# First waits tile by tile, attention's scores two tiles ahead, and the next head's q and k split early

## The chip, the core and the metric

The kernel runs on one core of one Trainium2 chip. The metric is the device time of one execution in microseconds (us). TensorE (PE in the profile) multiplies, VectorE (DVE), ScalarE (ACT) and GpSimd (POOL) work element by element, and SyncE (SP) issues nearly all DMAs. Each engine takes its instructions in the order in which they stand in its queue, and waits at an instruction until the semaphores that it names have been raised.

## What is computed

One inference step of a two-layer decoder: a gated linear attention (GLA) layer and a differential attention layer, each with a squared-ReLU MLP, for a prompt of 1024 tokens behind 16 meta tokens, and for eight running sequences with a paged cache of 4096 tokens each. The change is about the prompt's differential attention: eight heads, each with two score maps of depth 64 over the same values. Cut to that:

```python
def diff_core(q, k, v, q_pos, k_pos, lam):
    s = jnp.einsum('bqhmd,bkhmd->bhmqk', q, k).astype(F32) * (DIFF_DH ** -0.5)
    mask = k_pos[None, :] <= q_pos[:, None]
    s = jnp.where(mask, s, -jnp.inf)
    p = jax.nn.softmax(s, axis=-1)
    a = p[:, :, 0] - lam * p[:, :, 1]
    return jnp.einsum('bhqk,bkhe->bqhe', a, v.astype(F32))

def diff_prompt(x, w_in, lam, lam_init, g_sub, w_out):
    q, k, v = diff_project(x, w_in, pos)          # projections and partial rope
    ...                                           # diff_core, 128 queries at a time
    out = diff_output(o, g_sub, lam_init, w_out, x.dtype)   # rms_norm per head, then @ w_out
    return out, k.reshape(B, T, DIFF_HEADS, 2 * DIFF_DH), v
```

## The kernel before

**Stages.** In order of time: the GLA layer with the sample tokens' own path; the GLA output projection and the first MLP, beside which the running sequences' paged attention (`decode`, L861) goes on in the background; the projections of q, k and v (L1094 to L1136), still with `decode` beside them; the prompt's differential attention (L1142 to L1273); its output projection and the second MLP. Products keep fp32 accuracy by splitting each operand into a high and a low part (`split`, L194: a copy on ACT writes the high part, a subtraction on DVE or POOL the low one) and running three matmuls (`mm3`, L198). A weight tile comes by DMA into `raw` (L184), ACT casts it into `whi` (L186), and POOL subtracts into `wlo` (L187).

**Pools.** On-chip memory is handed out in pools that are opened and closed stage by stage on the same addresses. A tile's first user must wait for whoever used its memory before. With the default setting, that is everything that used the memory under the whole pool. `open_banks` (L125) does the same for the eight PSUM banks: three `mm`, three `ax` and two `sm` banks elsewhere, in attention two pairs `pr`, two `ax`, two `sm`. Attention opens `a1`, `a2`, `a3` and `scp` (L1144 to L1147) where `decode`'s page buffers (`pg`) and the projections' output buffers (`qo`) lay. Among their tiles are the mask `cmask`, two value tiles for the meta tokens `vm` that POOL clears (L1158), and five score tiles `as` of `scp`.

**One tile of attention** (`tile_`, L169) is 128 queries t = 0 to 7 of one head h against W = 16 + 128(t + 1) keys, in one to three chunks of at most 512 keys. Per chunk PE makes both score maps, three matmuls each (L1187), into a pair of PSUM banks; DVE adds the mask, scales, keeps the running minimum and writes to `as` (L1189), once per map. Over the whole width ACT takes the exponential with its sum (L1191, twice), DVE works out a reciprocal (L1193) and a factor (L1194) and combines the two maps (L1195). Then PE transposes 128 x 128 blocks (L1204, t + 2 of them), ACT copies them out (L1206), and PE multiplies with the values (L1209). A head is eight such tiles and 14 chunks; its next head's q and k are prepared by `prep` (L1075): 17 transposes of the reloaded rows (L1082, L1088), casts on ACT (L195), subtractions on DVE (L196). In a head the tiles come in the order 7, 1, 5, 3, 6, 0, 4, 2, and `prep` is advanced one step at tiles n = 1 to 4 of that order. `load_v` (L1160) loads the next head's values at n = 3, `load_qk` (L1065) the rows of the head after the next at n = 5. Every second head `o_norm` (L1213) scales finished outputs, in the last head `o_fm` (L1225) turns them for the output projection.

**What sets the order.** The program is written tile after tile; a scheduler puts each engine's instructions into a fixed order beforehand, so that some of tile n + 1's scores stand before tile n's transposes. On the chip each queue then runs in that order.

Of the kernel before, what the change touches and what calls it, by code (L numbers as in the profile page):

```python
# [25 lines left out]
NM = 16  # L26
# [9 lines left out]
PGB = 10  # L36
RUN = 4
HOLD = range(212, 228)
HTB = 1
# [72 lines left out]
def hybrid_step(ctx, tc, A, dbg=None, upto=9):  # L112
# [81 lines left out]
    def split(hi, lo, src, eng=V):  # L194
        S.copy(hi, src)  # L195
        return eng.tensor_tensor(lo, src, hi.bitcast(F32), op=ALU.subtract)  # L196
# [538 lines left out]
    kp = ctx.enter_context(tc.tile_pool(name="kp", bufs=1))  # L735
    de = ExitStack()
    dp = de.enter_context(tc.tile_pool(name="dp", bufs=1))
    dp2 = de.enter_context(tc.tile_pool(name="dp2", bufs=2))
    pgp = de.enter_context(tc.tile_pool(name="pgp", bufs=PGB))
# [297 lines left out]
    hp = e.enter_context(tc.tile_pool(name="hp", bufs=1))  # L1037
    ht = e.enter_context(tc.tile_pool(name="ht", bufs=HTB))
# [14 lines left out]
    rp = e.enter_context(tc.tile_pool(name="rp", bufs=1))  # L1053
    qt = e.enter_context(tc.tile_pool(name="qt", bufs=3))
    ht = e.enter_context(tc.tile_pool(name="qht", bufs=2))
# [7 lines left out]
    rqp = er.enter_context(tc.tile_pool(name="rqp", bufs=2, side="right"))  # L1063
# [80 lines left out]
    a1 = e.enter_context(tc.tile_pool(name="a1", bufs=1))  # L1144
    a2 = e.enter_context(tc.tile_pool(name="a2", bufs=4))
    a3 = e.enter_context(tc.tile_pool(name="a3", bufs=6))
    scp = e.enter_context(tc.tile_pool(name="scp", bufs=5))  # L1147
# [21 lines left out]
    def tile_(h, t, out, vm, vx, ks, qs):  # L1169
# [25 lines left out]
        V.scalar_tensor_tensor(sc_[:, 0, :W], sc_[:, 1, :W], neg[:, 0:1], sc_[:, 0, :W], ALU.mult, ALU.add)  # L1195

# [38 lines left out]
    vnxt = load_v(0)  # L1235
    for h in range(8):
        if h:
            head = hnxt
        vh = vnxt
        for n, t in enumerate((3, 2, 1, 0, 7, 6, 5, 4) if h == 7 else (7, 1, 5, 3, 6, 0, 4, 2)):  # L1240
            if h < 7:
                if n == 0:
                    nxt = prep(h + 1, *raws[h + 1])
                elif n < 5:
                    hnxt = next(nxt)
                if n == 3:
                    vnxt = load_v(h + 1)
# [6 lines left out]
            if n % 4 == 3:  # L1254
                ts = (slice(0, 4), slice(4, 8))[n // 4] if h == 7 else slice(t % 2, 8, 2)
                S.copy(Yd[:, ts, h], po.rearrange("p (t e) -> p t e", e=P))
                for i in range(4):
                    x = po[:, i * P : (i + 1) * P]
                    j = ts.start + i * (ts.step or 1)
                    S.activation(x, x, AF.Square, accum_out=oss[:, j, h : h + 1])  # L1260
            if n == 3 and h == 7:
                o_norm(slice(0, 4), slice(7, 8))
                for j in range(8):
                    o_fm(j, 0)
        if h < 6 and h % 2:
            o_norm(slice(0, 8), slice(h - 1, h + 1))
        elif h == 6:
            o_norm(slice(0, 8), slice(6, 7))
# [10 lines left out]
    hp = e.enter_context(tc.tile_pool(name="hp", bufs=1))  # L1279
    ht = e.enter_context(tc.tile_pool(name="ht", bufs=HTB))  # L1280
    rwp = e.enter_context(tc.tile_pool(name="rwp", bufs=5))
# [308 lines left out]
```

## Time and profile before

| | |
|---|---|
| median of 3 runs | 2869.12 us (2863.24, 2869.12, 2870.97) |
| the profiled execution | 2864.1 us, of which the span of its instructions is 2862.3 us |
| PE busy over the span | 2742.9 us, 96% |
| granted TensorE clock, mean | 0.987 |
| attention, first to last score reduction on DVE | 1785.02 to 2031.67 us |

Times in the trace count from the span's start. In rows of the timeline the columns are start, duration, engine (a q behind it is its queue of DMA issues), line, operation, tiles written and read, shape and count; the bracket holds the idle time of that engine before the row and what ended it. Rows of waits give the total, the number of times and the longest. Rows of windows give a stretch from start to end and its length, then the busy time of PE, PEld (loads of stationary operands), DVE, ACT and POOL with their instructions in brackets, the granted TensorE clock as a share of full speed, the DMA engines' busy share and GB/s. Ends of matmuls are modelled, so that a busy PE need not be a PE at its limit.

### The profile page before, as it was taken

How to read it: one execution, taken by the hardware profiler on the slowest of the kernel's cores; microseconds unless marked ns; L12 is line 12 of the kernel's file. 1: busy time of each engine (PE TensorE's matmuls, PEld its weight loads, DVE VectorE, ACT ScalarE, POOL GpSimd, SP SyncE). 2: the span in 40 equal slices, each digit the busy share in tenths (PEclk: the TensorE clock that was granted, in tenths of full speed). 3: DMA queues.
4: the chain of work that ended last, by engine and by line, in shares of the span. 5: the costliest groups of instructions: out<-in, count | busy, mean ns of one | idle time of the engine just before them, and what ended most of it. 6: DMA issues, size and time to landing. Idle time of an engine off the chain costs nothing.

```text
span 2862.3 us, 52240 instructions
## 1 busy us (share of the span) xinstructions
PE 2742.9 (96%) x19849; PEld 2244.1 (78%) x19849; DVE 1947.2 (68%) x3046; ACT 1095.1 (38%) x2229; POOL 1105.9 (39%) x744
## 2 busy tenths in 40 slices
PE   8889999999999999999999999888999999999997
PEld 5666667997777777777799978777889889797985
DVE  2565544568878787777668720788538887878788
ACT  3233344242221221221341112777615546355553
POOL 1221212233344343434233311000226767777774
PEclk9899999999999999999999999999999999999999
DMA  7557741634898898988669993111434555564584
GB/s 250 179 175 267 256 169 44 242 96 156 284 338 296 313 358 295 340 313 316 229 202 321 364 353 100 45 46 31 129 107 85 108 132 115 130 130 111 129 191 89
DMA packets 271833, 560.71 MB, mean 196 GB/s; under 512 B 23559, under 2 KB 138829, under 8 KB 267485
## 3 DMA queue, kind: packets, MB, share of 16 engines
q1 hardware_dynamic: 252284, 520.66, 53.2%
q0 software_dynamic: 19296, 36.71, 8.0%
q8 instruction: 156, 2.56, 0.4%
q14 instruction: 97, 0.79, 0.1%
HBM read 531.16 MB, written 29.26 MB: 196 GB/s over the span
## 4 chain that ended last, share of the span: by engine, by line
PE 74%; DVE 10%; DMA 6%; issue 4%; ACT 4%; POOL 1%; SPq 0%; DVEq 0%; POOLq 0%; ACTq 0%
PE mmt L199 18%; PE mmt L200 17%; PE mmt L201 17%; PE smt L843 4%; PE axt L199 3%; PE axt L200 3%; PE axt L201 3%; ACT as L1191 2%; DMA pg<-in_cache_k 1%; DMA swt<-in_mlp_w 1%; PE smt L519 1%; PE smt L1209 1%; DVE as L1189 1%; DVE Y L1506 1%; PE smt L1453 1%
## 5 line engine op out<-in xcount | busy, mean ns | idle before, releaser
L187 POOL TENSOR_TENSOR wlo<-raw,whi 128x512 fp32r<-128x512 f32 x256 | 365.4, 1440 | 769.9 <-ACT whi L186 688.6
L200 PE MATMUL mmt<-wlo,XH 128*128 128x256 f32 (+1 forms) x1760 | 526.3, 300 | 4.6 <-POOL wlo L187 4.6
L199 PE MATMUL mmt<-whi,XH 128*128 128x256 f32 (+1 forms) x1760 | 525.0, 301 | 4.6 <-ACT Y L323 3.6
L199 PE MATMUL mmt<-XH,whi 128*128 128x512 f32 (+1 forms) x1216 | 435.9, 359 | 5.1 <-DVE Y L913 3.0
L201 PE MATMUL mmt<-whi,XL 128*128 128x256 f32 x1536 | 436.7, 286 | 0.0
L201 PE MATMUL mmt<-XH,wlo 128*128 128x512 f32 (+1 forms) x1216 | 432.1, 356 | 0.0
L186 ACT CAST whi<-raw 128x512 fp32r<-128x512 f32 x256 | 153.0, 620 | 603.2 <-PE mmt L201 196.7
L200 PEld LDWEIGHTS mmt<-wlo,XH 128*128 128x128 f32 x1760 | 333.8, 190 | 32.3 <-issue 16.4
L803 DVE TENSOR_REDUCE sc<-pg 128x16 f32<-128x1024 f32 x256 | 308.3, 1212 | 72.4 <-POOL pg L802 69.8
L199 PEld LDWEIGHTS mmt<-whi,XH 128*128 128x128 f32 x1760 | 332.2, 190 | 30.8 <-issue 13.5
L802 DVE TENSOR_TENSOR pg<-pg,qb 128x1024 f32<-128x1024 f32 x192 | 267.3, 1399 | 62.1 <-DMA pg<-in_cache_k 52.1
L200 PE MATMUL mmt<-XL,whi 128*128 128x512 f32 x768 | 306.4, 399 | 0.0
L201 PEld LDWEIGHTS mmt<-whi,XL 128*128 128x128 f32 x1536 | 290.7, 190 | 8.7 <-issue 8.0
L199 PEld LDWEIGHTS mmt<-XH,whi 128*128 128x128 f32 x1216 | 229.7, 189 | 52.0 <-issue 12.9
L802 POOL TENSOR_TENSOR pg<-pg,qb 128x1024 f32<-128x1024 f32 x64 | 161.8, 2529 | 266.1 <-DMA pg<-in_cache_k 202.8
L201 PEld LDWEIGHTS mmt<-XH,wlo 128*128 128x128 f32 x1216 | 229.8, 189 | 34.4 <-issue 2.1
L199 PE MATMUL mmt<-whi,HH 128*128 128x512 f32 x512 | 205.1, 402 | 5.6 <-DVE Y L1027 5.2
L201 PE MATMUL mmt<-whi,HL 128*128 128x512 f32 x512 | 204.1, 399 | 0.0
L200 PE MATMUL mmt<-wlo,HH 128*128 128x512 f32 x512 | 203.6, 398 | 0.0
L1435 POOL TENSOR_TENSOR wlo<-RW,whi 128x512 fp32r<-128x512 f32 x96 | 173.6, 1843 | 49.1 <-ACT whi L1434 49.0
L1435 POOL TENSOR_TENSOR wlo<-rw,whi 128x512 fp32r<-128x512 f32 x92 | 157.2, 1747 | 77.7 <-ACT whi L1434 61.0
L200 PEld LDWEIGHTS mmt<-XL,whi 128*128 128x128 f32 x768 | 144.8, 189 | 38.1 <-issue 7.1
(424 smaller groups left out, 5695.0 us busy)
## 6 DMA issues: line engine op xcount, KB each, us to landing
pg<-in_cache_k SPq DMA_DIRECT2D x256, 512.0 KB, 5.7
pg<-in_cache_v SPq DMA_DIRECT2D x256, 512.0 KB, 6.4
raw<-in_mlp_w SPq DMA_DIRECT2D x164, 256.0 KB, 4.2
swt<-in_mlp_w SPq DMA_DIRECT2D x32, 1024.0 KB, 5.1
rw<-in_mlp_w SPq DMA_DIRECT2D x116, 256.0 KB, 3.5
RW<-in_mlp_w POOLq DMA_DIRECT2D x96, 256.0 KB, 5.7
raw<-in_gla_w_in SPq DMA_DIRECT2D x48, 256.0 KB, 3.5
swt<-in_gla_w_in SPq DMA_DIRECT2D x12, 1024.0 KB, 5.0
```

The source lines that it names most:

```text
L186: S.copy(hi[:, c], raw)
L187: G.tensor_tensor(lo[:, c], raw, hi[:, c].bitcast(F32), op=ALU.subtract)
L199: TE.matmul(ps, ah, bh, start=first, stop=False)
L200: TE.matmul(ps, ah, bl, start=False, stop=False)
L201: return TE.matmul(ps, al, bh, start=False, stop=last)
L519: TE.matmul(ps[o : o + TS, :], lhs[:, k + i, :], t[:, i, c * 512 : (c + 1) * 512], start=k == 0, stop=k == nk - 2)
L802: eng.tensor_tensor(pg, pg, qb, op=ALU.mult)
L803: return V.tensor_reduce(sc[:, n, :], pg.rearrange("p (h d) -> p h d", d=64), op=ALU.add, axis=AX.X).ins
L843: m = TE.matmul(acc[i * TS : i * TS + 16, :256], w[r, n, :], pg[r, i * 256 : (i + 1) * 256], start=n == 0, stop=n == NPG).ins
L1189: V.tensor_tensor_reduce(sc_[:, m, x:y], pss[m], mk, -0.125, -NEG if ci == 0 else mns[:, m : m + 1], ALU.add, ALU.min, mns[:, m : m + 1])
L1191: S.activation(sc_[:, m, :W], sc_[:, m, :W], AF.Exp, bias=mns[:, m : m + 1], scale=-1.0, accum_out=l[:, m : m + 1])
L1435: G.tensor_tensor(lo[:, k, :], t, hi[:, k, :].bitcast(F32), op=ALU.subtract)
```

## The change

Three edits. First, nearly every pool from the first `open_banks` on gets `reuse_waits="tile"`: a tile's first user waits only for those that used the memory under that tile. Second, `tile_` is cut into `front` (scores to L1195) and `back` (transposes and value products), and the loop over heads and tiles keeps two fronts ahead of the backs, across heads too. Third, `prep`'s four steps for q and k come in another order (both halves of k, then the second half of q, then the first), and are advanced one, one and two steps at n = 0, 1, 2 in place of one at each of n = 1 to 4. `load_v` and `load_qk` stay with n = 3 and n = 5 of the fronts.

```diff
-            banks[name] = banks["stack"].enter_context(tc.tile_pool(name=name, bufs=n, space=PSUM))
+            banks[name] = banks["stack"].enter_context(tc.tile_pool(name=name, bufs=n, space=PSUM, reuse_waits="tile"))
...
-    kp = ctx.enter_context(tc.tile_pool(name="kp", bufs=1))
+    kp = ctx.enter_context(tc.tile_pool(name="kp", bufs=1, reuse_waits="tile"))
...
-        for x, (hi, lo), at in ((kx, ks, NM), (qx, qs, 0)):
-            for c in range(2):
-                ps = axt()
-                for i in range(4):
-                    TE.transpose(ps[:, i * P : (i + 1) * P], x[:, 4 * c + i, :], ident)
-                cs = slice(at + 512 * c, at + 512 * c + 512)
-                split(hi[:, cs], lo[:, cs], ps)
-                yield ks, qs
+        for x, (hi, lo), at, c in ((kx, ks, NM, 0), (kx, ks, NM, 1), (qx, qs, 0, 1), (qx, qs, 0, 0)):
+            ps = axt()
+            for i in range(4):
+                TE.transpose(ps[:, i * P : (i + 1) * P], x[:, 4 * c + i, :], ident)
+            cs = slice(at + 512 * c, at + 512 * c + 512)
+            split(hi[:, cs], lo[:, cs], ps)
+            yield ks, qs
...
-    scp = e.enter_context(tc.tile_pool(name="scp", bufs=5))
+    scp = e.enter_context(tc.tile_pool(name="scp", bufs=5, reuse_waits="tile"))
...
-    def tile_(h, t, out, vm, vx, ks, qs):
+    def front(h, t, ks, qs):
...
+        return sc_
+
+    def back(t, sc_, out, vm, vx):
+
         keys = [(0, vm)] + [(NM + j * P, vx[:, j, :]) for j in range(t + 1)]
...
-    for h in range(8):
-        if h:
-            head = hnxt
-        vh = vnxt
-        for n, t in enumerate((3, 2, 1, 0, 7, 6, 5, 4) if h == 7 else (7, 1, 5, 3, 6, 0, 4, 2)):
+    heads, vals, todo = {0: head}, {0: load_v(0)}, []
+    steps = [(h, n, t) for h in range(8) for n, t in enumerate((3, 2, 1, 0, 7, 6, 5, 4) if h == 7 else (7, 1, 5, 3, 6, 0, 4, 2))]
+    for step in steps + [None] * 2:
+        if step:
+            h, n, t = step
             if h < 7:
                 if n == 0:
                     nxt = prep(h + 1, *raws[h + 1])
-                elif n < 5:
-                    hnxt = next(nxt)
+                for _ in range((1, 1, 2)[n] if n < 3 else 0):
+                    heads[h + 1] = next(nxt)
                 if n == 3:
-                    vnxt = load_v(h + 1)
+                    vals[h + 1] = load_v(h + 1)
                 elif n == 5 and h < 6:
                     raws.append(load_qk(h + 2))
-            if n % 4 == 0:
-                po = smt()
-            at = t % 4 if h == 7 else t // 2
-            tile_(h, t, po[:, at * P : (at + 1) * P], *vh, *head)
+            todo.append((step, front(h, t, *heads[h])))
+        if step and len(todo) <= 2:
+            continue
+        (h, n, t), sc_ = todo.pop(0)
+        if n % 4 == 0:
+            po = smt()
+        at = t % 4 if h == 7 else t // 2
+        back(t, sc_, po[:, at * P : (at + 1) * P], *vals[h])
```

Each engine issues as many instructions of each kind as before. Until the end of the projections their order is the same on every engine, and POOL's order is the same to the end; other waits stand at the first users of reopened pools. In the order of the change lines are shifted: L1187 is L1186 there, L1189 is L1188, L1158 is L1157, L1088 is L1087, L1204 is L1207 and L1209 is L1212.

**POOL, where attention's value tiles are cleared.** `vm` is cleared at L1158; the next L187 makes the low part of a weight tile for the projections. A name in the bracket is a semaphore: `SP_sequencer` is raised by SP's loads of page numbers (L769), `DMAHW` by DMAs, the others by engines. Before:

```order
L187 TENSOR_TENSOR wlo<-raw,whi 128x512 [waits DMAHW5_49,Activation_49]
L1158 MEMSET vm_21036 128x128 [waits DVE_49,SP_sequencer_49,PE_49,Pool_49]
L1158 MEMSET vm_21037 128x128
L187 TENSOR_TENSOR wlo<-raw,whi 128x512 [waits DMAHW1_49,Activation_49]
L834 MEMSET pg 32x1024 [waits DMAHW6_49,DMAHW7_49,DMAHW4_49,PE_49]
```

Now:

```order
L187 TENSOR_TENSOR wlo<-raw,whi 128x512 [waits DMAHW5_49,Activation_49]
L1157 MEMSET vm_21036 128x128 [waits DVE_49,Pool_49]
L1157 MEMSET vm_21037 128x128
L187 TENSOR_TENSOR wlo<-raw,whi 128x512 [waits DMAHW1_49,Activation_49]
L834 MEMSET pg 32x1024 [waits DMAHW6_49,DMAHW7_49,DMAHW4_49,PE_49]
```

The order is the same; the clearing of `vm` no longer waits for SP and PE, and its wait for DVE is one for the last product with a page buffer (L802) in place of one for the last softmax of `decode` (L824).

**DVE, where attention begins.** The rows are the splits of head 0 (into `XL_85`), of head 1 (into `XL_86`), and the first reductions of scores. Before:

```order
L196 TENSOR_TENSOR XL_85<-axt,XH_83 128x16 [waits Activation_49]
L196 TENSOR_TENSOR XL_85<-axt,XH_83 128x512 [waits Activation_49] x4
L1189 ISA as,ast<-prt,cmask 128x352 [waits DMAHW2_49,DMAHW3_49,DMAHW1_49,DMAHW4_49,DMAHW0_49,DMAHW5_49,DVE_49,DMAHW6_49,PE_49,DMAHW7_49,Activation_49,Pool_49]
L1189 ISA ast 128x1
L1189 ISA as,ast<-prt,cmask 128x352
```

Now:

```order
L196 TENSOR_TENSOR XL_85<-axt,XH_83 128x16 [waits Activation_49]
L196 TENSOR_TENSOR XL_85<-axt,XH_83 128x512 [waits Activation_49] x4
L196 TENSOR_TENSOR XL_86<-axt,XH_84 128x16 [waits Activation_49]
L196 TENSOR_TENSOR XL_86<-axt,XH_84 128x512 [waits Activation_49]
L1188 ISA as,ast<-prt,cmask 128x352 [waits DMAHW3_49,DMAHW4_49,DMAHW2_49,DMAHW5_49,DMAHW1_49,DMAHW7_49,DVE_49,PE_49]
L1188 ISA ast 128x1
L1188 ISA as,ast<-prt,cmask 128x352
```

Of the waits of the first reduction, those for ACT and POOL are gone, and those for DMAs are now for loads of `decode`'s pages, none for the writes of `qo`. Two of head 1's five subtractions stand ahead of it, the other three among the first reductions.

**PE, from one head to the next.** `prt` holds scores (`128x352` is the first tile of the next head), `axt<-c_ident,as` are transposes of a finished tile, `smt` value products, `axt<-c_ident,rqk` the transposes of `prep`. Before, behind the last scores of the old head:

```order
L1204 MATMUL axt<-c_ident,as 128x128 x7
L1209 MATMUL smt<-vm_21037,aT 128x128
L1209 MATMUL smt<-whi,aT 128x128 x3
L1088 MATMUL axt<-c_ident,rqk 128x128 x4
L1209 MATMUL smt<-whi,aT 128x128 x3
L1204 MATMUL axt<-c_ident,as 128x128 x5
L1209 MATMUL smt<-vm_21037,aT 128x128
L1209 MATMUL smt<-whi,aT 128x128 x3
L1088 MATMUL axt<-c_ident,rqk 128x128 x4
L1209 MATMUL smt<-whi,aT 128x128
L1204 MATMUL axt<-c_ident,as 128x128 x4
L1187 MATMUL prt<-XH_83 128x352 x2
```

Now, from the last scores of the old head on:

```order
L1186 MATMUL prt<-XH_84 128x400 x2
L1186 MATMUL prt<-XL_86,XH_84 128x400 x2
L1186 MATMUL prt<-XH_84,XL_86 128x400 x2
L1212 MATMUL smt<-vm_21037,aT 128x128
L1212 MATMUL smt<-whi,aT 128x128 x3
L1207 MATMUL axt<-c_ident,as 128x128 x4
L1186 MATMUL prt<-XH_83 128x352 x2
L1186 MATMUL prt<-XL_85,XH_83 128x352 x2
L1186 MATMUL prt<-XH_83,XL_85 128x352 x2
```

Eight transposes and products stand between the old head's last scores and the new head's first, and none of `prep`'s transposes, which now stand among the first three tiles of each head.

More of the change, by code (lines that the diff above doesn't have):

```diff
@@ L1036, in hybrid_step @@
     e = ExitStack()
-    hp = e.enter_context(tc.tile_pool(name="hp", bufs=1))
-    ht = e.enter_context(tc.tile_pool(name="ht", bufs=HTB))
+    hp = e.enter_context(tc.tile_pool(name="hp", bufs=1, reuse_waits="tile"))
+    ht = e.enter_context(tc.tile_pool(name="ht", bufs=HTB, reuse_waits="tile"))
     HH = hp.tile([P, 4, T], F32R, name="HH")
@@ L1052, in hybrid_step @@
     e = ExitStack()
-    rp = e.enter_context(tc.tile_pool(name="rp", bufs=1))
-    qt = e.enter_context(tc.tile_pool(name="qt", bufs=3))
-    ht = e.enter_context(tc.tile_pool(name="qht", bufs=2))
+    rp = e.enter_context(tc.tile_pool(name="rp", bufs=1, reuse_waits="tile"))
+    qt = e.enter_context(tc.tile_pool(name="qt", bufs=3, reuse_waits="tile"))
+    ht = e.enter_context(tc.tile_pool(name="qht", bufs=2, reuse_waits="tile"))
     gs = kp.tile([P, 1], F32, name="gs")
@@ L1062, in hybrid_step @@
     er = ExitStack()
-    rqp = er.enter_context(tc.tile_pool(name="rqp", bufs=2, side="right"))
+    rqp = er.enter_context(tc.tile_pool(name="rqp", bufs=2, side="right", reuse_waits="tile"))
     def load_qk(h):
@@ L1243, in hybrid_step @@
                     nxt = prep(h + 1, *raws[h + 1])
-                elif n < 5:
-                    hnxt = next(nxt)
+                for _ in range((1, 1, 2)[n] if n < 3 else 0):
+                    heads[h + 1] = next(nxt)
                 if n == 3:
-                    vnxt = load_v(h + 1)
+                    vals[h + 1] = load_v(h + 1)
                 elif n == 5 and h < 6:
                     raws.append(load_qk(h + 2))
-            if n % 4 == 0:
-                po = smt()
-            at = t % 4 if h == 7 else t // 2
-            tile_(h, t, po[:, at * P : (at + 1) * P], *vh, *head)
[L1254 to L1265, printed above, removed]
+            todo.append((step, front(h, t, *heads[h])))
[6 more added lines that the diff above has]
+        back(t, sc_, po[:, at * P : (at + 1) * P], *vals[h])
+        if n % 4 == 3:
+            ts = (slice(0, 4), slice(4, 8))[n // 4] if h == 7 else slice(t % 2, 8, 2)
+            S.copy(Yd[:, ts, h], po.rearrange("p (t e) -> p t e", e=P))
+            for i in range(4):
+                x = po[:, i * P : (i + 1) * P]
+                j = ts.start + i * (ts.step or 1)
+                S.activation(x, x, AF.Square, accum_out=oss[:, j, h : h + 1])
+        if n == 3 and h == 7:
+            o_norm(slice(0, 4), slice(7, 8))
+            for j in range(8):
+                o_fm(j, 0)
+        elif n == 7 and h < 6 and h % 2:
             o_norm(slice(0, 8), slice(h - 1, h + 1))
-        elif h == 6:
+        elif n == 7 and h == 6:
             o_norm(slice(0, 8), slice(6, 7))
@@ L1278, in hybrid_step @@
     e = ExitStack()
-    hp = e.enter_context(tc.tile_pool(name="hp", bufs=1))
-    ht = e.enter_context(tc.tile_pool(name="ht", bufs=HTB))
-    rwp = e.enter_context(tc.tile_pool(name="rwp", bufs=5))
+    hp = e.enter_context(tc.tile_pool(name="hp", bufs=1, reuse_waits="tile"))
+    ht = e.enter_context(tc.tile_pool(name="ht", bufs=HTB, reuse_waits="tile"))
+    rwp = e.enter_context(tc.tile_pool(name="rwp", bufs=5, reuse_waits="tile"))
     for c in range(2):
```

13 lines of the change are left out of this document (6 added, 7 removed).

## The prediction

> **What bounds the kernel now.** I read the page's busy times first, then windows of the stages, then the waits of each engine in attention, and last the timelines around the places where PE stands still.
>
> ```profile
> PE 2742.9 (96%) x19849; PEld 2244.1 (78%) x19849; DVE 1947.2 (68%) x3046; ACT 1095.1 (38%) x2229; POOL 1105.9 (39%) x744
> ```
>
> PE is busy 96% of the span: only 119 us of the 2862.3 could be won by letting it wait less. Windows show that attention is another regime than the stages around it:
>
> ```profile
> 1708.00:1712.00 4.00, 4.00 (x39) 2.89 (x38) 0.00 (x0) 0.30 (x1) 0.84 (x1) 1.00 1.00 352
> ...
> 1772.00:1776.00 4.00, 4.00 (x35) 4.00 (x35) 0.04 (x1) 0.59 (x1) 0.00 (x0) 1.00 1.07 285
> ...
> 1815.58:1847.06 31.48, 28.59 (x235) 23.20 (x233) 24.35 (x87) 24.43 (x70) 0.00 (x0) 1.00 0.20 53
> 1847.06:1879.08 32.02, 28.51 (x235) 23.19 (x233) 26.57 (x90) 24.19 (x70) 2.90 (x1) 1.00 0.19 50
> ```
>
> In the projections PE leaves no gap: the first two rows are the first and the last of 17 windows of 4 us, each with 4.00 of PE. The other two rows are a head each, from one first score reduction to the next: DVE works 25.5 us of 31.75 on average, ACT 24.3. PE's 28.5 are flattered, since the modelled end of a matmul lies well behind the start of the next: a row below has six value products in 0.83 us though one alone lasts 0.28. So three engines hand work round and none is full; where DVE waits in attention (1785 to 2024 us) is what a longer lead can remove:
>
> ```profile
> DVE as L1189 <- PE prt L1187: 20.7, 21, 1.5
> DVE ast L1193 <- ACT as L1191: 13.8, 20, 1.3
> DVE as L1189 <- DMA out_v_rows_p<-qo: 13.0, 1, 13.0
> DVE XL L196 <- ACT XH L195: 8.7, 11, 1.7
> DVE orr L1218 <- ACT as L1191: 1.2, 4, 0.3
> ```
>
> Leaving out the 13.0, which is the wait before the first reduction, this is 20.7 + 13.8 + 8.7 + 1.2 = 44.4 us.
>
> **The change part by part. First, the wait of POOL before attention (pool edit).**
>
> ```profile
> 1703.51 0.34 POOL L1158 MEMSET vm<- 128x128 f32 x2 [9.38 <-SPq L769]
> 1703.82 1.26 POOL L187 TENSOR_TENSOR wlo<-raw,whi 128x512 fp32r<-128x512 f32 x1
> ...
> 1705.14 0.58 PE L200 MATMUL mmt<-wlo,XH 128*128 128x256 f32 x1 [3.15 <-POOL wlo L187]
> 1705.52 0.41 PE L201 MATMUL mmt<-whi,XL 128*128 128x256 f32 x1
> 1705.73 0.42 PE L199 MATMUL mmt<-whi,XH 128*128 128x256 f32 x1
> ...
> 1704.00:1708.00 4.00, 2.86 (x13) 2.87 (x14) 0.00 (x0) 0.00 (x0) 1.08 (x1) 0.57 1.05 370
> ```
>
> POOL stands 9.38 us at the clearing of `vm`, for SP's load of the last page number; the weight tile queued behind it comes late, and PE stands 3.15 us. With that wait for SP gone, POOL clears `vm` before and makes the tile as soon as ACT has cast it:
>
> ```profile
> 1695.99 0.62 ACT L186 CAST whi<-raw 128x512 fp32r<-128x512 f32 x1 [3.21 <-DMA raw<-in_diff_w_in]
> ```
>
> 1695.99 + 0.62 + 1.26 = 1697.9 us, four before PE wants it. The stall also halves the clock (0.57 in that window): its 13 matmuls start 0.21 us apart where the same kind elsewhere starts 0.12 apart, 1.2 us more.
>
> ```profile
> 1740.22 0.28 PE L201 MATMUL mmt<-whi,XL 128*128 128x256 f32 x1
> 1740.34 0.28 PE L199 MATMUL mmt<-whi,XH 128*128 128x256 f32 x1
> ```
>
> Gain 3.15 + 1.2 = **4.4 us**; bounds 0 (another late tile or page takes its place) and 4.5. In the 17 full windows from 1708 on the later tiles come in time, at a pace that PE itself sets by freeing buffers, so I let the gain carry through.
>
> [...]
>
> **Second, the first score reduction (pool edit).**
>
> ```profile
> 1779.83 0.43 PE L1187 MATMUL prt<-XH 64*128 64x352 f32 x2 [0.72 <-ACT qo L1108]
> 1780.73 0.33 PE L1187 MATMUL prt<-XH,XL 64*128 64x352 f32 x2
> 1786.05 0.65 PE L1187 MATMUL prt<-XH 64*128 64x336 f32 x2 [5.00 <-DVE ast L1189]
> ...
> 1785.02 0.53 DVE L1189 CUSTOM_DVE_ANT_0 as<-prt,cmask 128x352 f32<-128x352 f32 x1 [12.98 <-DMA out_v_rows_p<-qo]
> ```
>
> The scores lie ready at 1780.73 + 0.33 = 1781.1, but the reduction writes into memory of the pool that held `qo`, and waits for the last write of `qo` to land, until 1785.02. With waits by tile it needs the pages' loads, long landed, and PE. Gain 1785.0 - 1781.1 = **3.9 us**; bounds 0 and 4.7 (PE's own 0.72 goes too). Two of head 1's subtractions now stand ahead, 0.15 + 0.69 us, but they are work that DVE has to do anyway, and PE's five transposes of them (0.55 us) replace the 0.72 gap.
>
> **Third, the passage between heads (order of `prep`, two fronts ahead).** One of them on DVE and PE:
>
> ```profile
> 1840.43 0.57 DVE L1189 CUSTOM_DVE_ANT_0 as<-prt,cmask 128x400 f32<-128x400 f32 x1
> 1845.13 0.69 DVE L196 TENSOR_TENSOR XL<-axt,XH 128x512 fp32r<-128x512 f32 x1 [1.66 <-ACT XH L195]
> 1847.06 0.52 DVE L1189 CUSTOM_DVE_ANT_0 as<-prt,cmask 128x352 f32<-128x352 f32 x1 [1.23 <-PE prt L1187]
> 1850.52 0.57 DVE L1189 CUSTOM_DVE_ANT_0 as<-prt,cmask,ast 128x336 f32<-128x336 f32 x1 [1.47 <-PE prt L1187]
> 1853.83 0.17 DVE L1193 RECIPROCAL ast<-ls 128x1 f32<-128x1 f32 x1 [1.07 <-ACT as L1191]
> ...
> 1843.21 0.83 PE L1209 MATMUL smt<-whi,aT 128*128 128x128 f32 x6
> 1845.15 0.43 PE L1187 MATMUL prt<-XH 64*128 64x352 f32 x2
> ```
>
> Between the old head's last scores and the new head's first PE has 43 transposes and products (some 0.11 us each, 4.8 us) and waits among them for splits and copies; DVE, out of scores, waits 1.66 + 1.23 + 1.47 + 1.07 us there. In the new order only eight such matmuls (0.9 us) stand there, and q and k are split a half head earlier. What stays, row by row: of the 13.8 us for exponentials about half, 7, because in every second head the reciprocal still stands right behind the second tile's scores; of the 20.7 for scores a third, 7, because each chunk needs one of two PSUM pairs back; of the splits' 8.7, 2; of 1.2, 1. Kept 17, gained 44.4 - 17 = **27 us**. Bounds: 13 (only the splits and a little of the scores go) and 44.4 (DVE never waits). A head then takes 31.75 - 27 / 7.5 = 28.1 us, with DVE at 91% and ACT at 86%, nearly as full as between two passages now.
>
> Everything else of these two edits I cost at nothing. The same transposes, casts and subtractions are issued, only sooner. SP now holds the small key load of the head after the next ahead of the next head's values, both behind PE; their data are wanted most of a head (some 28 us) later, and a load of this size lands in 6.3 us:
>
> ```profile
> rqk<-out_k_rows_p SPq DMA_DIRECT2D x8, 512.0 KB, 6.3
> ```
>
> If that cover were gone, each late load would stop all of attention for its landing time.
>
> **Fourth, the passage out of attention (pool edit).**
>
> ```profile
> 2029.73 1.09 PE L1229 MATMUL axt<-c_ident,Y 128*128 128x128 f32 x4 [2.22 <-DVE XL L1231]
> 2031.81 0.55 PE L199 MATMUL mmt<-whi,XH 128*128 128x256 f32 x1 [0.99 <-DVE ast L1189]
> ```
>
> The projection's first matmul waits for the last score reduction only because of its bank's pool; by tile the wait moves to the eighth. Gain **0.9 us**, bounds 0 and 2 (if the clock, which falls here too, stays up). The 2.22 is a data dependence and stays. The other reopened pools (start of `decode`, MLPs, projections) shed waits at places where PE shows no gap that they end: nothing; a wait of SP's that goes there only lets loads run ahead of a PE that is full.
>
> **Sum:** 4.4 + 3.9 + 27 + 0.9 = 36 us. The profiled execution took 2864.1, so 2828; it lies 5.0 below the median of 2869.1, and I do not know which the next runs resemble, so I add half of that: **2830 us**. By bounds: all small 13, giving 2851 to 2856; all large 4.5 + 4.7 + 44.4 + 2 = 56, giving 2808 to 2813.
>
> **Rivals.** (a) *DVE becomes the bound without a rest*: the 44.4 go whole, 4.4 + 3.9 + 44.4 + 0.9 = 54 us, 2813. For it speaks that DVE has almost no idle time between two passages; against it ACT, at 24.3 us a head, which would have to follow at 96% of DVE's 25.5 in a fixed order. (b) *ACT and DVE block each other*: casts of the next head now stand in ACT's queue between the long exponentials of a head's first, widest tiles, and only 10 of the expected 27 are left: 4.4 + 3.9 + 10 = 18 us, 2848. For it: ACT's 24.3 us are close to DVE's. Against: these tiles have two tiles' lead. (c) *The edit of the pools and the lead change no wait that decides*, since the scheduler already put scores ahead: within 0.3%, 2867. Against: the waits that go are named in the rows. (d) *Slower: the two PSUM pairs become the bound.* PE now meets scores two tiles early; if their pair is still unread, PE stops, and old tiles' transposes and products behind it in its queue stop with it, so ACT's copies and the outputs come late. A stop costs the two reductions of a chunk, 2 x 0.57 = 1.15 us. Against the 8.3 us of the first two terms and 8.6 for 0.3%, it decides from 15 such stops in the 64 tiles on; at one in every second tile it is 32 x 1.15 - 8.3 = 28 us slower, 2897. Today PE so waits ten times only:
>
> ```profile
> PE prt L1187 <- DVE ast L1189: 12.5, 10, 5.0
> ```
>
> That is 7.5 us without the 5.0 at the start, and most scores in the new order still have transposes and products between them, which speaks against (d). [...]
>
> **Chances.** My forecast 0.55 (its own range 2820 to 2841), (a) 0.11, (b) 0.18, (c) 0.05, (d) 0.11. The range that takes in most of (a) and (b), and the case of all small bounds, is 2812 to 2855. What a measurement of this kernel can tell from no change is about 0.3%, 8.6 us. The forecast, (a) and (b) are faster by more: 0.84; within it 0.05; slower 0.11.
>
> **What would show it.** Right: no bracket at `vm`'s clearing, and PE without a gap near 1702; the first reduction some 8 us earlier (4.4 + 3.9, near 1777) and waiting for PE; heads of about 28 us with DVE near 25.5 busy; waits of DVE in attention near 17 us, with `L196 <- L195` nearly gone; stages behind attention as long as before, only earlier. Wrong: heads of 31 us with the waits under other names, PE waiting for reductions (L1188) far more than ten times, or a gap of PE before 1779 that takes the place of the one removed.

## The result, and the profile after

| | before | changed |
|---|---|---|
| median of 9 runs | 2869.12 us (2863.24 to 2874.82) | 2857.94 us (2850.05 to 2862.96) |
| the profiled execution, of which the span | 2864.1, 2862.3 us | 2860.1, 2858.4 us |
| attention, first score reduction to the end of the last | 246.6 us | 247.4 us |

The ratio is 0.9968, 95% interval 0.9956 to 0.998: between 6 and 13 us faster, where 39 were forecast; 2857.9 lies above the stated range of 2812 to 2855. Of the kernels compared below, the one with the pools alone had one execution of 4085.8 us at a granted clock of 0.61, which its median leaves out. The two profiles, cut at the starts of the same matmuls and reductions, say where:

| stretch | before | changed | difference |
|---|---|---|---|
| start to 1677.6 (order of all engines unchanged) | 1677.63 | 1680.33 | +2.7 |
| the next 400 matmuls, with the clearing of `vm` | 45.06 | 40.53 | -4.5 |
| from there to the first score reduction | 62.33 | 58.43 | -3.9 |
| attention | 246.64 | 247.43 | +0.8 |
| end of the last reduction to matmul 15200, in the output projection | 78.63 | 76.96 | -1.7 |
| to matmul 18000, in the second MLP | 427.50 | 425.91 | -1.6 |
| 400 matmuls of the second MLP | 49.28 | 53.55 | +4.3 |
| rest of the span | 275.2 | 275.3 | 0 |

The first row is no effect that can be tied to an edit: in the other kernels it lay between 3 us less and 16 us more than before. The timeline of POOL in the changed kernel (columns as before) shows the first term: `vm` is cleared at once, without a bracket. The rows of windows below it have PE full, at full clock, where 3.15 us were lost (before 1705.14 there, which is about 1707.8 here).

```profile
1695.99 1.27 POOL L187 TENSOR_TENSOR wlo<-raw,whi 128x512 fp32r<-128x512 f32 x1 [9.46 <-ACT whi L186]
1697.21 0.34 POOL L1157 MEMSET vm<- 128x128 f32 x2
```

```profile
1700.00:1704.00 4.00, 4.00 (x37) 2.81 (x37) 0.00 (x0) 0.00 (x0) 1.13 (x1) 1.00 1.00 353
1704.00:1708.00 4.00, 4.00 (x40) 2.96 (x39) 0.33 (x1) 0.00 (x0) 0.00 (x0) 1.00 0.99 392
```

The first reduction no longer waits for a DMA; DVE's timeline has it right behind a subtraction of head 1's preparation:

```profile
1778.68 0.69 DVE L196 TENSOR_TENSOR XL<-axt,XH 128x512 fp32r<-128x512 f32 x1 [0.45 <-ACT XH L195]
1779.29 0.51 DVE L1188 CUSTOM_DVE_ANT_0 as<-prt,cmask 128x352 f32<-128x352 f32 x1
```

Attention is another story. Windows of the changed kernel from one head's first reduction to the next's, for heads 1, 2 and 3:

```profile
1805.70:1833.09 27.39, 25.97 (x215) 20.62 (x213) 25.14 (x90) 23.70 (x69) 0.00 (x0) 1.00 0.21 59
1833.09:1866.51 33.42, 29.06 (x235) 24.52 (x233) 24.96 (x85) 23.03 (x63) 2.90 (x1) 0.95 0.18 49
1866.51:1898.49 31.98, 28.68 (x237) 23.34 (x235) 26.39 (x92) 26.23 (x76) 0.00 (x0) 1.00 0.20 51
```

Heads 0 and 1 take 26.4 and 27.4 us, as short as hoped; then heads of 33.4, 32.0, 33.2, 32.0 and 34.4 us follow, with the same work. DVE's waits in attention (total, times, longest) show what became of the 44.4 us before:

```profile
DVE ast L1192 <- ACT as L1190: 19.4, 21, 2.2
DVE as L1188 <- PE prt L1186: 11.2, 15, 1.3
DVE as L1188 <- PE axt L1207: 9.3, 12, 1.8
DVE Y L1226 <- POOL orr L1223: 2.0, 1, 2.0
DVE XL L196 <- ACT XH L195: 1.4, 5, 0.5
DVE orr L1221 <- ACT as L1190: 0.6, 3, 0.2
```

They add up to 43.9, nearly what the prediction had before (44.4, to 2024 us; what falls behind that is 0.3). The waits for the splits went from 8.7 to 1.4, as the edit intends; those for exponentials grew from 13.8 to 19.4, and reductions now also wait for PE at a transpose (9.3), which means that PE's queue stood at one. Where, a stretch of head 4 shows, in the timelines of ACT, PE and DVE:

```profile
1951.45 1.06 ACT L1190 ACTIVATE as<-as,ast 128x912 f32<-128x912 f32 x1
...
1952.50 0.57 ACT L195 CAST XH<-axt 128x512 fp32r<-128x512 f32 x1
...
1953.25 0.57 ACT L1209 COPY aT<-axt 128x512 f32<-128x512 f32 x1
```

```profile
1951.84 0.66 PE L1207 MATMUL axt<-c_ident,as 128*128 128x128 f32 x4 [0.55 <-DVE XL L196]
1953.88 0.66 PE L1207 MATMUL axt<-c_ident,as 128*128 128x128 f32 x4 [1.39 <-ACT aT L1209]
```

```profile
1951.10 0.68 DVE L196 TENSOR_TENSOR XL<-axt,XH 128x512 fp32r<-128x512 f32 x1
1955.57 0.31 DVE L1188 CUSTOM_DVE_ANT_0 as<-prt,cmask 128x144 f32<-128x144 f32 x1 [0.73 <-PE axt L1207]
1956.95 0.51 DVE L1188 CUSTOM_DVE_ANT_0 as<-prt,cmask 128x336 f32<-128x336 f32 x1 [0.84 <-PE axt L1207]
```

The transposes of the scores want one of the two `ax` banks. One is held by the preparation until DVE's subtraction ends at 1951.78, the other until ACT's copy ends at 1953.82, and that copy stands in ACT's queue behind an exponential, a cast of the next head and a square (0.27 us, in the rows left out). PE stands 0.55 and 1.39 us, and the reductions behind it come late.

The +4.3 in the second MLP goes with one instruction, an addition that is 5.5 us longer. In the changed kernel's timeline and then in that of before, the same addition on DVE, and what POOL does meanwhile:

```profile
2512.98 7.52 DVE L1416 TENSOR_TENSOR RX<-XR,RX 128x1032 f32<-128x1032 f32 x1
...
2513.13 4.10 POOL L1441 TENSOR_TENSOR wlo<-RW,whi 128x512 fp32r<-128x512 f32 x3
```

```profile
2520.36 6.30 POOL L1435 TENSOR_TENSOR wlo<-RW,whi 128x512 fp32r<-128x512 f32 x3
...
2521.27 2.00 DVE L1410 TENSOR_TENSOR RX<-XR,RX 128x1032 f32<-128x1032 f32 x1
```

There DVE took 2.00 us and POOL's three subtractions 6.30; now POOL takes 4.10 for them and DVE 7.52 for the addition.

### The profile page after: what moved, and what is told of

Same layout as the page of the kernel before. It is cut to its first block, busy times and chain, and to the rows that moved or that the text cites. A ratio compares the mean times of both kernels' runs of the same rounds, so it can differ in the third digit from the quotient of the medians.

```text
span 2858.4 us, 52228 instructions
## 1 busy us (share of the span) xinstructions
PE 2742.7 (96%) x19849; PEld 2243.9 (79%) x19849; DVE 1954.1 (68%) x3046; ACT 1096.5 (38%) x2229; POOL 1105.3 (39%) x744
## 5 line engine op out<-in xcount | busy, mean ns | idle before, releaser
L187 POOL TENSOR_TENSOR wlo<-raw,whi 128x512 fp32r<-128x512 f32 x256 | 369.7, 1457 | 770.4 <-ACT whi L186 691.5
L802 DVE TENSOR_TENSOR pg<-pg,qb 128x1024 f32<-128x1024 f32 x192 | 263.9, 1382 | 63.1 <-DMA pg<-in_cache_k 52.6
L802 POOL TENSOR_TENSOR pg<-pg,qb 128x1024 f32<-128x1024 f32 x64 | 160.9, 2515 | 262.8 <-DMA pg<-in_cache_k 196.1
```

Source lines behind the costliest of these rows:

```text
L187: G.tensor_tensor(lo[:, c], raw, hi[:, c].bitcast(F32), op=ALU.subtract)
L802: eng.tensor_tensor(pg, pg, qb, op=ALU.mult)
```

## The experiments

Lengths of attention (first score reduction to the end of the last, in the profile) are compared between kernels; each is from one profile. Times of whole kernels are medians of several runs, or a single one where "one run" is said. The preparation's four steps stand at fronts n of a head; a back of tile n is written two tiles later where two fronts are ahead.

**The edits one by one.** The first three kernels go back to before's loop, order or pace (the loop over `steps` then also ends without its two empty steps):

```diff
 # pools alone; the third kernel has only this hunk
-        if step and len(todo) <= 2:
+        if step and len(todo) <= 0:
 # pools alone, and two ahead: the old order of q's halves, and
-                for _ in range((1, 1, 2)[n] if n < 3 else 0):
+                if 1 <= n < 5:
                     heads[h + 1] = next(nxt)
```

> The pools' edit alone: waits by tile everywhere, attention's loop and the preparation of the next head as before. Theory A (the whole measured gain comes from the pools, the other two edits give nothing): PE's gap near 1702 is gone (about 4.5 us), the first score reduction waits for PE instead of a write (about 4 us), attention from the first to the end of the last reduction stays 246 to 248 us, total about 8 to 9 us under before. Rival B (the pools give little, the lead gives the rest): total within 4 us of before.

> Pools by tile and two fronts ahead; order and pace of the next head's preparation as before (k, k, q, q at the second to fifth tile). Theory C (the early preparation is what cost the gain: its transposes share the two ax banks with those of the scores): attention falls to 220 to 230 us, total 2832 to 2842. Rival D (the lead itself only moves the waits, ACT's copies stand behind the exponentials of tiles two ahead): attention 243 to 251 us, total within 5 us of the changed kernel.

> Pools by tile and the early preparation, no front ahead of its back. Theory C (early preparation costs): attention 250 us or more, longer than with the pools alone. Rival D (the lead is what costs): attention shorter than with the pools alone, by the waits for q and k at the passages, 225 to 240 us, total 2840 to 2852.

| | attention | total | ratio to before |
|---|---|---|---|
| pools alone | 247.5 us | 2860.2 us | 0.9963 [0.9950, 0.9976] |
| pools, two ahead, old preparation | 236.2 us | 2848.0 us | 0.9921 [0.9904, 0.9938] |
| pools, early preparation, none ahead | 245.0 us | 2860.8 us | 0.9965 [0.9951, 0.9979] |
| the change (all three) | 247.4 us | 2857.9 us | 0.9968 [0.9956, 0.9980] |

The pools give all that the change gives (A). Their kernel has before's order of attention: in heads 1 to 6 the rows of PE, DVE, ACT and POOL are the same one by one, and each head is as long as before to 0.1 us. Its profile had a granted clock of 0.95 outside the falls (0.938 over the span), where all others had 1.00 (0.982 to 0.990 over the span), which did not show in these heads. Differences of several us between lengths of attention are therefore more than chance. Two fronts ahead with the old preparation shorten attention by 11 us, and the early preparation takes them back: C points the right way, but its 220 to 230 us were not reached, and without a lead the early preparation does a little good, not harm: 245.0 lies between what C and D expected. What it harms depends on where the preparation then comes to stand. Heads 2 and 3 of the kernel with two fronts ahead and the old preparation, in windows:

```profile
1829.45:1859.93 30.48, 28.70 (x237) 23.66 (x239) 25.20 (x89) 23.19 (x66) 2.90 (x1) 1.00 0.20 53
1859.93:1889.80 29.87, 28.36 (x235) 23.05 (x232) 24.95 (x90) 25.53 (x74) 0.00 (x0) 1.00 0.20 55
```

**The lead itself does nothing.** Two fronts ahead with the four steps at n = 3 to 6, so that they stand where they stood before relative to the backs, gave the same order with the same waits as the pools alone, row for row on all five engines. It was therefore not run. The scheduler had put the scores that far ahead already; writing fronts two tiles early only moves the preparation forward by two tiles relative to the backs. So the attention of the kernels so far differs by the place of the preparation alone. What the preparation costs at all was measured by leaving it out, with two fronts ahead and with none (the pace is cut in the same way):

```diff
-                if n == 0:
+                if h and n == 0:
+                    heads[h + 1] = heads[h - 1]
+                elif n == 0:
                     nxt = prep(h + 1, *raws[h + 1])
...
```

> The changed kernel, but from head 2 on nothing is prepared: head h takes q and k of head h - 2, so 17 transposes, 5 casts and 5 subtractions per head are left out. Theory C (the preparation between the tiles makes the waits): heads 2 to 6 from first to first reduction take 24 to 27 us, nearly what DVE has to do (about 22). Rival D (the lead blocks the queues by itself): heads still 29 us or more.

> Pools by tile, no front ahead, and from head 2 on nothing is prepared (head h takes q and k of head h - 2; 17 transposes, 5 casts and 5 subtractions per head are left out). The lead written in the program turned out to change nothing where the preparation stands at the same place relative to the backs: the scheduler gives the same order row for row. Theory E (only the place of the preparation counts, not the lead): heads 2 to 6 take what they take in the changed kernel without preparation, 26 to 27 us on average. Rival D (the lead matters where nothing is prepared): 29 us or more.

Without preparation heads 2 to 6 take 26.5 us on average in the changed kernel, and 26.5 with the pools alone: E holds. It had to, since the rows of the two traces come in one order there, but for one small instruction of DVE: the lead itself changes nothing. In heads 2 to 5, which take 26.7 us without it, the preparation costs 31.8 - 26.7 = 5.1 us a head before, 32.6 - 26.7 = 5.9 in the changed kernel, and 30.2 - 26.7 = 3.5 with the steps at n = 1 to 4. One head without it, with the pools alone, as a window:

```profile
1896.50:1923.10 26.60, 26.60 (x227) 22.04 (x225) 23.95 (x87) 22.75 (x66) 2.90 (x1) 1.00 0.08 22
```

PE has no gap in it. Since ends of matmuls are modelled, that alone would not show PE at its limit; the chain of work that ended last says the same: from 1844 to 1911 us (heads 2, 3 and half of 4), 62% of it are rows of PE, 29% of ACT and 8% of DVE. Over heads 1 to 5 before the same chain had 25% of PE, 37% of ACT and 35% of DVE. Without preparation it is mostly PE that sets a head's length, not DVE.

**Order, pace and place.** Four kernels with two fronts ahead; the first, third and fourth have the change's order of the halves, the second the old one:

```diff
 # the steps, in place of the change's n = 0, 1, 2, 2
-                for _ in range((1, 1, 2)[n] if n < 3 else 0):
+                for _ in range((1, 2, 3, 4).count(n)):     # or (0, 2, 4, 6), (0, 1, 2, 3), (1, 2, 3, 3)
```

> The changed kernel with the old pace (one step at each of the tiles n = 1 to 4), so that only the order of the two halves of q differs from the run with two fronts ahead and the old preparation. Theory E (the place in time counts, the order of the halves does not): total 2845 to 2851, heads near 30.2 us. Rival F (the new order of the halves costs): nearer to the changed kernel, 2854 to 2860.

> Two fronts ahead, old order of the halves, the four steps spread over the head (n = 0, 2, 4, 6). Theory G (steps close together crowd the two ax banks; spread ones find a free bank): heads 29 us or less, total 2836 to 2845. Rival H (what counts is that the last step is done well before the passage; with the fourth at n = 6 the passage waits come back): heads 30.5 us or more, total 2850 to 2860.

> The changed kernel with its four steps at n = 0, 1, 2, 3, one each: as early as the change, but without two steps on one tile. The kernel with n = 1 to 4 had attention 236.6 us long, the changed one (n = 0, 1, 2, 2) 247.4. Theory I (the earlier place costs: the preparation stands before transposes and copies of old tiles): attention 243 us or more. Theory J (two steps at once crowd the two ax banks): 239 us or less.

> The changed kernel with its four steps one tile later, n = 1, 2, 3, 3: two steps on one tile, but later. Theory I (earliness costs): attention 239 us or less. Theory J (the double step costs): 243 us or more.

| steps at n | order of q's halves | attention | total |
|---|---|---|---|
| 1, 2, 3, 4 | old | 236.2 us | 2848.0 us |
| 1, 2, 3, 4 | new | 236.6 us | 2851.1 us |
| 0, 2, 4, 6 | old | 240.6 us | 2851.2 us |
| 0, 1, 2, 3 | new | 243.2 us | 2855.7 us (one run) |
| 1, 2, 3, 3 | new | 242.5 us | 2853.0 us (one run) |
| 0, 1, 2, 2 (the change) | new | 247.4 us | 2857.9 us |
| 3, 4, 5, 6 (the order of the pools alone) | old | 247.5 us | 2860.2 us |

The order of the halves costs next to nothing (E, against F). One tile earlier costs 6.6 us of attention, two steps on one tile 5.9, both together 10.8: neither I nor J is the whole, both have a part (each from one profile; 242.5 lies just short of J's 243). Later than n = 1 to 4 costs as much as earlier. Spreading the steps over the whole head is no way out: 30.9 us a head and 2851.2 in total are H's numbers, not G's; whether for H's reason was not looked into.

**The banks.** The transposes of the preparation and those of the scores share the two `ax` banks. PE's waits at the scores' transposes for a copy or a subtraction, before and with two fronts ahead and the old preparation:

```profile
PE axt L1204 <- ACT aT L1206: 7.3, 6, 1.4
PE axt L1204 <- DVE XL L196: 5.4, 6, 1.1
```

```profile
PE axt L1208 <- ACT aT L1210: 2.0, 3, 0.7
PE axt L1208 <- DVE XL L196: 0.7, 1, 0.7
```

The sums are 12.7 us before and 2.7 there; in the changed kernel, below, the sum is 14.0. So the change did not take these waits away, and the later place of the preparation (n = 1 to 4) did, with attention 11 us shorter. Not every place follows this: with steps at n = 1, 2, 3, 3 and at 0, 2, 4, 6 the sums are only 3.3 and 2.5, and attention is 4 to 6 us longer than at 1 to 4 for reasons that stay open. A third bank, at the price of one of the two output banks:

```diff
-    open_banks(pr=2, ax=2, sm=2)
+    open_banks(pr=2, ax=3, sm=1)
```

> The changed kernel with three ax banks and one sm bank in attention. Theory L (its mid-head waits come from two ax banks): attention from 247.4 to 238 us or less, and PE's waits of 14.5 us for copies and subtractions at the transposes of scores fall under 5. Rival (the banks do not matter, the time is work in an unlucky order; or the single output bank, whose squares on ACT must be done before the next value products, takes their place): 245 us or more.

> The pools alone with three ax banks and one sm bank. Theory L, where the old place of the preparation collides less with the two banks: attention changes by less than 5 us from 247.5. Rival (a third bank helps at any place): 238 us or less.

The changed kernel with three banks: attention 235.8 us, 11.6 less, total 2845.6 in one run. PE's longest waits in attention, first in the changed kernel, then with three banks (L1209 is here ACT's copy of the transposed scores):

```profile
PE axt L1207 <- ACT aT L1209: 7.9, 5, 2.0
PE smt L1212 <- ACT aT L1209: 6.4, 13, 0.8
PE axt L1207 <- DVE XL L196: 6.1, 8, 1.0
PE prt L1186 <- DVE ast L1188: 3.2, 6, 0.9
```

```profile
PE prt L1186 <- DVE ast L1188: 8.2, 11, 1.6
PE axt L1232 <- DVE XL L1234: 2.6, 1, 2.6
PE axt L1207 <- ACT aT L1209: 1.8, 4, 0.7
PE axt L1087 <- ACT aT L1209: 1.1, 3, 0.6
```

The waits of the scores' transposes for a copy or a subtraction, 7.9 + 6.1 us, fall to 1.8: L holds. With the old place of the preparation the third bank does harm: the pools alone go from 247.5 to 268.3 us, neither what L nor its rival expected. There DVE waits 51.7 us for scores up to 2025 us, and ACT 23.9 at its copies of the outputs; with two banks it was 31.4 and 1.2 (8.6 of DVE's wait lies ahead of attention in both):

```profile
DVE as L1189 <- PE prt L1187: 51.7, 19, 8.6
ACT Y L1263 <- PE smt L1213: 23.9, 7, 4.1
```

```profile
DVE as L1189 <- PE prt L1187: 31.4, 23, 8.6
ACT Y L1263 <- PE smt L1213: 1.2, 1, 1.2
```

So the single output bank is the likely reason, less by its squares, for which PE waits only 0.9 us, than by where the copies now stand in ACT's queue; that was not tried apart. The granted clock is also at one half for 44 us of this attention (0.982 over the span), against 10 with two banks; in the prediction's stall matmuls started 0.21 us apart at that clock in place of 0.12, so this lengthens it too.

**Which engine is next.** Two ahead with the old preparation, and work moved to POOL, which was busy for 15.4 of the 247 us of attention before:

```diff
 # scaling on POOL
-            V.tensor_tensor(Yd[:, a, hs], Yd[:, a, hs], bc(...), op=ALU.mult)
+            (G if hs.stop < 8 else V).tensor_tensor(Yd[:, a, hs], Yd[:, a, hs], bc(...), op=ALU.mult)
 # sums of squares of heads 0 to 6 on POOL, too (ACT keeps head 7)
+                y = Yd[:, ts, h]
+                G.tensor_tensor(sq, y, y, op=ALU.mult)
+                w = P // 2
+                while w > 1:
+                    G.tensor_tensor(sq[:, :, :w], sq[:, :, :w], sq[:, :, w : 2 * w], op=ALU.add)
+                    w //= 2
+                G.tensor_tensor(oss[:, ts, h : h + 1], sq[:, :, 0:1], sq[:, :, 1:2], op=ALU.add)
```

> Two fronts ahead with the old preparation, and o_norm's scaling of the outputs of heads 0 to 6 on POOL in place of DVE (14 multiplications of 0.68 us leave DVE). If DVE's load sets the pace of a head: attention 8 to 10 us shorter than without this edit, total near 2839. If the waits between the queues set it: less than 3 us.

> Two fronts ahead, old preparation, scaling of heads 0 to 6 on POOL as in the run before, and the sums of squares of heads 0 to 6 too: POOL squares the copied outputs and adds them by halves, in place of 56 squares on ACT, 0.46 us each, 25.8 us that leave ACT's queue (3.7 us a head). Theory K (copies wait in ACT's queue behind this work): attention 232.3 minus 10 to 20 us, 212 to 222 us, total 2825 to 2835. Rival (DVE and PE set the pace of a head now): attention 228 us or more, total 2840 or more.

> The kernel with squares on POOL, and PSUM shared out as three ax banks and one sm bank in place of two and two. If the two ax banks (the preparation's transposes and those of the scores) are what queues meet at: attention 5 to 15 us shorter than with two. If the single output bank makes the value products wait for the copy of the old outputs: 5 us or more longer.

> Two fronts ahead, old preparation, scaling on POOL, squares on ACT, three ax banks and one sm bank. If the third bank made the gain of the run with squares on POOL and three banks (attention 227.4 us): 224 to 230 us. If the gain needs the squares off ACT, since they hold the single output bank: 234 us or more.

> The changed kernel's early preparation (n = 0, 1, 2, 2) with scaling and squares on POOL and three ax banks. Theory L (early preparation costs only through the two banks): attention 225 to 230 us, as with the old preparation (227.4). Rival (earliness costs by itself): 233 us or more.

| two ahead, scaling on POOL, and | attention | total | ratio to before |
|---|---|---|---|
| two `ax` banks, squares on ACT | 232.3 us | 2844.2 us | 0.9919 [0.9887, 0.9951] |
| two `ax` banks, squares on POOL | 240.9 us | 2855.3 us | 0.9941 [0.9924, 0.9957] |
| three `ax` banks, squares on ACT | 236.3 us | 2841.2 us | 0.9892 [0.9870, 0.9915] |
| three `ax` banks, squares on POOL | 227.4 us | 2834.6 us | 0.9878 [0.9858, 0.9898] |
| the same, early preparation | 230.3 us | 2834.1 us | 0.9866 [0.9842, 0.9891] |

Taking 9.5 us (14 x 0.68) from DVE gave 3.9: DVE alone does not set the pace. Taking 26 us from ACT at two banks gave nothing, and made attention 8.6 us longer and the whole 11: K falls; why it got longer stays open. A third bank with the squares on ACT gave nothing for attention either. Both together gave 4.9 us of attention over the first row, probably since the single output bank is then free as soon as it is copied; heads 2 and 3 of this kernel as windows:

```profile
1832.80:1860.48 27.68, 27.00 (x228) 22.37 (x228) 24.35 (x89) 21.04 (x53) 14.31 (x21) 1.00 0.21 59
1860.48:1889.59 29.11, 28.81 (x244) 24.24 (x241) 24.64 (x85) 22.49 (x55) 8.81 (x17) 1.00 0.21 56
```

PE is busy for 55.81 of these 56.79 us, and its rows are 77% of the chain that ended last over heads 1 to 5. With three banks and the squares on POOL the early preparation costs 2.9 us of attention in place of 10.8, and nothing of the total; 230.3 lies just above L's 230. These two kernels are the fastest found, 35 us under before. In the profile of the first, 19 of them lie in attention, 8 ahead of it and 6 from its end into the second MLP. The addition of the second MLP that took 7.52 us in the changed kernel takes about 2 us or less in them, as before (2.00).

## Why the prediction was wrong

**First term (POOL before attention), right.** 4.4 forecast, 4.5 measured, and every run with waits by tile has that stretch at 40.5 us to within 0.4. **Second (first reduction), right.** 3.9 forecast, 3.9 measured. The reduction came at 1779.3 instead of "near 1777", which is the 2.7 us by which this execution was late before; it stands behind a subtraction of head 1 there, not behind PE.

**Third (passages), wrong: 27 forecast, -0.8 measured.** Two steps of it failed.

"The same transposes, casts and subtractions are issued, only sooner", and so at nothing. They are no free filling where they went: between a bank's first transpose and its release stand a cast on ACT and a subtraction on DVE, in queues full of exponentials and reductions, and the scores' transposes need the same two banks. What left the passage came back in the middle of the head: 43.9 us of waits of DVE in place of 44.4, and 14.0 us of PE at the scores' transposes in place of 12.7. The third bank, with which these 14.0 fall to 1.8 and attention by 11.6, and the steps at n = 1 to 4, with 2.7 and 11.2 less, show it.

"Kept 17, gained 27" took DVE's idle time for what a better order could return, down to heads of 28.1 us, after calling PE's 28.5 busy microseconds a head flattered. They were nearly right: in the kernel with three banks and the squares on POOL, where PE makes up 77% of the chain, the same work keeps it busy for 27.9 us a head. So 28.1 was about PE's floor, to be had only with nothing else in the way, and not a middle value; heads 1 to 5 of that kernel average 28.6. The forecast also gave the lead a share; the scheduler had the scores ahead already, and the lead's only effect was to place the preparation two tiles earlier. Its count of the passage was short as well, though no term rests on it: a product with the values makes two rows of the trace, so that the 43 are 58 rows or 6.4 us at 0.11, not 4.8, and the eight that stay are 12 in every second head and 19 in the others.

**Fourth (out of attention), right in kind.** 0.9 forecast, 1.7 measured, inside its bounds of 0 and 2. The gap of 0.99 us is gone, but how much of the 1.7 the pools made is not shown: with the pools alone, where that gap is gone too, the stretch took 79.0 us (at the granted clock of 0.95). **The stages behind, costed at nothing,** gave -1.6 and +4.3: "stages behind attention as long as before" did not hold: one addition of DVE in the second MLP took 7.52 us in place of 2.00. With the differences of the profile's stretches, the first one left out, -4.5 - 3.9 + 0.8 - 1.7 - 1.6 + 4.3 = -6.6 us, inside the measured 6 to 13.

**The rivals.** (b), copies and casts between exponentials in ACT's queue, is what the timeline shows at the stall, but with nothing left of the gain instead of 10 us, and through the banks: taking the squares off ACT did not help by itself. (c) had one half right, that the scheduler has the scores ahead. (d) did not come: PE waits 3.2 us for reductions, less than the 7.5 before. Nor did DVE and ACT stop together before: of the 5.8 us for which DVE idles at the passage shown (1843 to 1855 us), ACT idles only 1.9 with it. (a) would need heads of 25.8 us, less than the 26.7 that they take on average without any preparation, with PE rather than DVE in the way.

## What to carry to other kernels

Before work is moved earlier, count the buffers it passes through and who else needs them: here a transpose's bank was held until the readers in ACT's and DVE's queues were done, for which PE stood 0.55 and 1.39 us in the stretch shown, and two steps on one tile cost 5.9 us of attention. A wait named at a passage is a gain only if the engine with the least slack has room for it; find that floor first, by leaving the suspect work out; here PE's busy time was near it (28.5 us a head before, 27.9 in the kernel with three banks and the squares on POOL). Where a scheduler orders the queues, compare the orders of each edit by itself before giving it a share: here an edit that looked like the main one changed no row of its own.

## What was not expected of the hardware

The addition that took 7.52 us takes 1.22 at its shortest among the 16 of its kind. It took over 7 us in all twelve kernels (the changed one among them) that need 53 to 54 us for those 400 matmuls, and about 2 or less in the four that need 49 to 50, before among them (the two without preparation have other counts). Its 7.52 us lie beside three subtractions of POOL, the DMA issues and a subtraction behind them, and end at 2520.5. The 7.52 - 1.22 = 6.3 us by which it is longer are more than any single instruction of POOL there took (three subtractions took 4.10 together). The addition starts at 2512.98, the first of the subtractions at 2513.13, though starts on POOL are rough; what makes the addition long is not shown.

In the changed kernel's head 2 the clock fell to half for 3.4 us behind a gap of PE of only 2.0 us (the longest of its waits for ACT's copies above): 1 - 0.5 x 3.4 / 33.4 is the 0.95 of that head's window. In the prediction's case the gap was 3.15 us. It fell in heads 4 and 6, too, where no gap of the 8 us ahead was over 0.86 us; these three heads are the longest, 33.2 to 34.4 us, where heads 3 and 5 take 32.0. The stretches ahead of the three falls, each as long as the fall itself (3.41 us), as windows:

```profile
1853.53:1856.94 3.41, 1.43 (x14) 1.20 (x12) 2.30 (x5) 3.35 (x13) 0.00 (x0) 1.00 1.07 292
1908.15:1911.56 3.41, 1.80 (x15) 1.16 (x14) 3.29 (x15) 2.71 (x7) 0.00 (x0) 1.00 0.03 7
1973.00:1976.41 3.41, 2.02 (x18) 1.19 (x16) 3.29 (x13) 2.71 (x6) 0.00 (x0) 1.00 0.00 0
```

PE was busy for 1.43, 1.80 and 2.02 us of them. So the clock fell here behind several short waits, in heads 4 and 6 none over 0.86 us, as well as behind one longer gap.
